# Moving a hybrid trunk's activation transfers to GpSimd's queue, its low halves and sums to VectorE, and its second modulation into the first feed-forward sweep

## The chip, the cores and the metric

One core of a Trainium2 chip runs the kernel: TensorE (matmuls, PE in the profile, with PEld for its weight loads), VectorE (DVE), ScalarE (ACT), GpSimd (POOL) and SyncE (SP), an on-chip memory of 128 partitions, eight matmul result banks, and a memory off the chip that transfers (DMA) reach. A transfer is issued by an engine's queue, in the order of that queue's program; an engine that comes to an instruction whose data or buffer is not ready waits, and with it all that stands behind. The metric is the device time of one execution in microseconds (us), the median of several.

## What is computed

Two layers over 1024 latent tokens and 256 context tokens of width 1024, all in fp32. Layer 0 mixes tokens by a convolution module, layer 1 by grouped-query attention (16 heads, 4 key heads); each is followed by a SwiGLU feed-forward part of width 2816. Each part is normalised before and after, and scaled, shifted and gated by a modulation: a linear map of SiLU(c) for latent tokens, of SiLU(c_ctx) for context tokens, six blocks of 1024 numbers per layer.

```
for i in range(2):
    mod_x = silu(c) @ w_mod[i] + b_mod[i]          # six blocks: sh, sc, g, shf, scf, gf
    mod_c = silu(c_ctx) @ w_mod[i] + b_mod[i]
    hx = rmsnorm(x, g0) * (1 + sc_x) + sh_x        # the same for ctx
    yx = conv_module(hx) if i == 0 else attention(hx, hc)
    x  = x + g_x * rmsnorm(yx, g1)                 # ctx too, in layer 0
    fx = rmsnorm(x, g2) * (1 + scf_x) + shf_x
    x  = x + gf_x * rmsnorm((silu(fx @ w1) * (fx @ w3)) @ w2, g3)
```

## The kernel before

**Data.** Activations stand with features on partitions and tokens along them, as 8 blocks of 128 features. The 1280 tokens form three pieces: C (256 context tokens), L and R (512 latent tokens each). A product of two fp32 matrices is made of three: each operand is split into a high half (rounded to fp32r) and a low half (the rest), and `mm3` (L149, its matmuls in L155, L156 and L157) adds high x high, high x low and low x high.

**Weights.** `wload` (L125) fetches a block of 128 x 1024 weights (512 KB) into one of two `wr` buffers over SP's queue, has ScalarE write the high half (`wh`, L132), and VectorE (L136) or GpSimd (L138) the low half (`wl`); there are three `wh` and three `wl`. `lo_dve` is the share of the low halves that goes to VectorE: 0 at the start, 1 from L914 on (convolution, layer norm, first feed-forward sweep), 0.5 from L1011 on, to the end of the kernel. Small tiles have rings too: `sb` of four buffers, `sm` of three; the halves of keys and queries lie in `sb` until their store has gone out.

**Transfers.** Nearly all are issued by SP, weights and activations in one queue: residual loads (L542), stores of the residual stream x1, x2, x3 and the output (L567, L990), keys (L731: 8 stores of a piece, each of 32 rows for 4 key heads), queries (L757: 4 stores per pair of projections), key loads (L763), query loads (L770, two buffers), attention results (L1048, and their loads L1079), cosines and sines (L726, L727), and the modulation's weights (L238). ScalarE issues some of the convolution's.

**Order of the work.** The program is written as generators; a foreground loop yields an estimate of its time, and `pump(budget)` lets generators in the background queue `bgq` issue as many steps as their own yields fit into that budget. So the order on each engine is largely that of the program. The stages:

1. Modulation of layer 0 (scale and shift by TensorE, the other 32 blocks by VectorE products beside the projections, `mod_dve`, L225), first normalisation, pointwise projections and the convolution, to about 385 us.
2. Layer norm, second pointwise projection, residual and second normalisation of C, L and R (`ln`, `pw2`, `post_pre`), to about 600 us.
3. First feed-forward sweep, over C and L together (L981): 22 up-steps with w1 and w3, and down-steps with w2 after each group of four. `pp("R")`, R's residual and normalisation, runs in its background. Matmul results have banks 0 to 4 and 7, statistics 5 and 6.
4. Second sweep, over R (L1012), with `early()` in the background: residuals of C and L, layer 1's modulation (all 48 blocks, `mod_dve` in room from the tiles T2 and T3), normalisation and keys and values of C, normalisation of L.
5. Handover: L's keys, values and queries beside R's residual and normalisation (L1015 to L1025), then R's keys, values and first query pair (L1026 to L1030). The first scores need all keys of a head back from off-chip memory.
6. Attention (`attn_stream`): per unit of a key head and 128 queries scores (L784), softmax numerators (L790 on VectorE, L792 on ScalarE), transposes (L802), halves (L805, L806) and values (L808, L809). At first R's other three query pairs run beside it; the second half of the units runs beside the output projection and the feed-forward sweep over L (L1111).
7. Output projection and feed-forward sweep over R (L1118), and the tail: the last residuals and the stores of the output.

**Sums.** `post` (L534) applies norm and gate to each of 8 feature blocks (VectorE, L550) and adds the residual (L553). `aid` names the blocks whose add goes to GpSimd: 6 of 8 in the handover, 4 of 8 from there on. `rsqrt` (L277) is a chain of small VectorE operations.

Of the kernel before, what the change touches and what calls it, by code (L numbers as in the profile page):

```python
# [15 lines left out]
P = 128  # L16
# [38 lines left out]
class Kern:  # L55
    def __init__(self, tc, es, a):
# [14 lines left out]
        self.aid = ()  # L71
# [153 lines left out]
    def mod_dve(self, l, fs, cr, raws, junk):  # L225


        nc = self.nc
        if l:
            self.cond_row(cr)  # L230

        def load(i):
            if i >= len(fs):
                return None
            raw = raws[i % len(raws)]
            if raw is None:
# [12 lines left out]
        for s in range(2 if l else 0):  # L249
            m = self.mod[l][s][:, 0:16 if s else 48]  # L250
            nc.vector.tensor_tensor(m, m, self.c["bmod"][:, l, 0:16 if s else 48], op=ALU.add)

    def mod_room(self, *tags):
        t = [self.T(g, [P, {"HS": 5312, "KB": 2656}.get(g, 4096)]) for g in tags]
        parts = [u[:, i:i + 1024] for u in t for i in range(2048 if u is t[0] else 0, u.shape[1] - 1023, 1024)]
        return t[0][:, 0:2048].rearrange("p (s d) -> p s d", s=2), parts[1:], parts[0]
# [277 lines left out]
    def post(self, l, i, y, yacc, xsrc, c0, segs, sink, xtag, kind="st"):  # L534
# [6 lines left out]
        def load(q):  # L541
            nc.sync.dma_start(xr[:, q % m:q % m + 2, :], xsrc[:, q:q + 2, c0:c0 + n])  # L542
# [4 lines left out]
        for k in range(KT):  # L547
# [5 lines left out]
            (nc.gpsimd if k in self.aid else nc.vector).tensor_tensor(yk, yk, xr[:, k % m, :], op=ALU.add)  # L553
# [5 lines left out]
    def post_pre(self, l, y, yacc, xsrc, xdst, c0, c1, dcol, xtag, ftags, box):  # L559
# [18 lines left out]
    def ffn(self, l, fs, ytags, htags, boxes, tanh=False, parts=1):  # L578
# [5 lines left out]
        ys = [self.T(t, [P, KT, n]) for t, n in zip(ytags, ns)]  # L584
# [135 lines left out]
    def qkv(self, h, col0, n, wk, want_q=True):  # L720
# [4 lines left out]
        if want_q:  # L725
            nc.sync.dma_start(wk[:, 0, :n], a["cos"][:, lat0:lat0 + n])  # L726
            nc.sync.dma_start(wk[:, 1, :n], a["sin"][:, lat0:lat0 + n])  # L727

        def ksink(i, v):
            for r in (i % 2, i % 2 + 2):  # L730
                nc.sync.dma_start(self.ksd[:, 32 * r:32 * r + 32, i // 2, col0:col0 + n], v)  # L731
# [19 lines left out]
        if want_q:  # L751
            for t in range(NKV):
# [4 lines left out]
                             lambda i, v: nc.sync.dma_start(  # L757
# [4 lines left out]
    def load_k(self, t, kt, c0=0, c1=TOK):  # L762
        self.nc.sync.dma_start(kt.bitcast(F32).rearrange("p (a t) -> p a t", a=2)[:, :, c0:c1],  # L763
                               self.ksd[t, :, :, c0:c1])

    def load_q(self, t, qt):
# [3 lines left out]
        nc.sync.dma_start(q, self.qsd[t, :, :, qt * P:(qt + 1) * P])  # L770
# [88 lines left out]
    def build(self):  # L859
# [70 lines left out]
        modg = self.mod_dve(0, range(16, 48), cr, (mraw, None), self.ps[:, 5:7].rearrange("p a b -> p (a b)"))  # L930
# [20 lines left out]
        for s in range(2):  # L951
            nc.vector.tensor_tensor(self.mod[0][s][:, 16:48], self.mod[0][s][:, 16:48], c["bmod"][:, 0, 16:48],
                                    op=ALU.add)
        self.derive(0, (1, 2, 3))
# [26 lines left out]
        for us in self.ffn(0, [(fv["C"][0], CTX), (fv["L"][0], 512)], ("HR", "T5"), ("KB", "HS"),  # L981
                           (zv["C"], zv["L"])):
            self.pump(us)
        self.drain()

        def final(l, y, src, dst, c0, c1, dcol, xtag, kind="st"):
            segs = segs_of(c0, c1)

            def sink(k):
                nc.sync.dma_start(dst[:, k, c0 - dcol:c1 - dcol], y[0][:, k, :])  # L990
# [20 lines left out]
        self.lo_dve = 0.5  # L1011
# [7 lines left out]
        self.aid = (1, 2, 3, 5, 6, 7)  # L1019
# [4 lines left out]
        self.aid = (1, 3, 5, 7)  # L1024
# [8 lines left out]
    def attention(self, final, qr):  # L1033
# [9 lines left out]
        def dst(q0):  # L1043
            def of(t, q):
                st = self.sb(256).rearrange("p (a q) -> p a q", q=P)

                def done():
                    nc.sync.dma_start(self.od[:, 2 * t:2 * t + 2, q * P:(q + 1) * P], st)  # L1048
# [175 lines left out]
```

## Time and profile before

| what | value |
|---|---|
| median of 3 runs | 3185.4 us (3184.72 to 3186.8) |
| the profiled execution | 3188.66 us; its span 3186.8 us |
| mean granted TensorE clock | 0.956 of full speed |
| TensorE busy | 2954.3 us, 93% (weight loads 2461.8) |
| VectorE busy | 1899.3 us, 60% |
| ScalarE busy | 1193.6 us, 37% |
| GpSimd busy | 352.9 us, 11%, 188 instructions |
| moved by SP's and ScalarE's queue | 328.91 MB, 31.8% of 16 engines' span |

How to read the rows: a group of instructions has its line, engine, operation, the tiles written and read (`wl<-wr,wh`), its count, then busy time and mean ns of one, then the engine's idle time just before them and what ended it. A timeline row has start and duration in us, and in brackets the idle time before it with what ended it (`<-DVE sm L683`: the end of VectorE's instruction in L683 that wrote `sm`). `SPq` is SP's queue; a merged row of it (x8) reaches from the first issue to the last. A window's row gives start and end, its length, the busy time of the five engines with their instructions, the granted clock, the DMA engines' mean share and GB/s. Times are from the span's start.

### The profile page before, as it was taken

To read this page: it belongs to the slowest core of one execution; us is meant where nothing else is said; L and a number is where in the kernel's file an instruction comes from. 1 tells how busy PE (TensorE), PEld (TensorE's weight loads), DVE (VectorE), ACT (ScalarE), POOL (GpSimd) and SP (SyncE) were. 2 spreads that over 40 slices of the span, in tenths; PEclk is the share of its full clock that TensorE was granted. 3 is DMA by queue.
4 is the path that set the end of the run, shared out by engine and by line. 5 is a ranking of instruction groups with operands and counts; after the bars stand their busy time and mean duration, and the time that the engine had idled before them with its cause. 6 is when DMAs were issued, how large, how long until landed. Compare 5 with 4: busy or idle time off the path is not lost. (4 is left out here: it accounts for less than half of the span.)

```text
span 3186.8 us, 39120 instructions
## 1 busy us (share of the span) xinstructions
PE 2954.3 (93%) x15210; PEld 2461.8 (77%) x15210; DVE 1899.3 (60%) x3026; ACT 1193.6 (37%) x1879; POOL 352.9 (11%) x188
## 2 busy tenths in 40 slices
PE   7899979899999999989966899989999999899997
PEld 5799878688888878778755677767777778778886
DVE  5877567742333379755564789866566653653335
ACT  5221245432111133233232588754545543332222
POOL 0000000000000012212221100021111112222222
PEclk9999959899999999999988899999999999899998
DMA  6544324322121257523334311222122133342332
GB/s 227 155 122 106 106 58 140 135 76 67 60 66 60 66 178 261 215 93 106 119 110 136 138 44 62 72 86 78 58 83 75 60 114 99 129 143 93 93 99 73
DMA packets 170425, 339.50 MB, mean 107 GB/s; under 512 B 30336, under 2 KB 83584, under 8 KB 169088
## 3 DMA queue, kind: packets, MB, share of 16 engines
q1 hardware_dynamic: 144128, 328.91, 31.8%
q10 hardware_dynamic: 26112, 8.10, 1.1%
q8 instruction: 119, 1.95, 0.3%
q14 instruction: 66, 0.54, 0.1%
HBM read 289.76 MB, written 41.81 MB: 104 GB/s over the span
## 5 line engine op out<-in xcount | busy, mean ns | idle before, releaser
L157 PE MATMUL ps<-T,wl 128*128 128x512 f32 (+1 forms) x2256 | 852.7, 378 | 33.9 <-DVE wl L136 32.6
L155 PE MATMUL ps<-T,wh 128*128 128x512 f32 (+1 forms) x2256 | 853.4, 379 | 9.2 <-ACT wh L132 7.0
L156 PE MATMUL ps<-T,wh 128*128 128x512 f32 (+1 forms) x2192 | 823.6, 376 | 1.8 <-DVE T L147 1.8
L132 ACT CAST wh<-wr 128x1024 fp32r<-128x1024 f32 x348 | 365.3, 1050 | 1098.1 <-PE ps L156 865.3
L138 POOL TENSOR_TENSOR wl<-wr,wh 128x1024 fp32r<-128x1024 f32 x123 | 301.5, 2452 | 2432.1 <-ACT wh L132 2232.2
L157 PEld LDWEIGHTS ps<-T,wl 128*128 128x128 f32 x2256 | 432.9, 192 | 113.5 <-DVE wl L136 35.4
L136 DVE TENSOR_TENSOR wl<-wr,wh 128x1024 fp32r<-128x1024 f32 x225 | 282.0, 1254 | 396.1 <-ACT wh L132 389.0
L155 PEld LDWEIGHTS ps<-T,wh 128*128 128x128 f32 x2256 | 432.4, 192 | 85.7 <-ACT wh L132 7.7
L156 PEld LDWEIGHTS ps<-T,wh 128*128 128x128 f32 x2192 | 419.5, 191 | 76.1 <-DVE T L147 3.3
L156 PE MATMUL ps<-HS,wh 128*128 128x512 f32 (+1 forms) x784 | 308.6, 394 | 3.0 <-DVE HS L147 3.0
L806 DVE TENSOR_TENSOR T<-ps,T 128x512 fp32r<-128x512 f32 x320 | 216.8, 687 | 126.4 <-ACT T L805 125.8
L157 PE MATMUL ps<-HS,wl 128*128 128x512 f32 (+1 forms) x720 | 281.5, 392 | 3.0 <-DVE wl L136 3.0
L155 PE MATMUL ps<-HS,wh 128*128 128x512 f32 (+1 forms) x720 | 281.6, 393 | 2.3 <-DVE sm L615 2.2
L805 ACT CAST T<-ps 128x512 fp32r<-128x512 f32 x320 | 185.9, 585 | 194.7 <-PE ps L802 170.5
L802 PE MATMUL ps<-cst,T 128*128 128x128 f32 x1100 | 193.2, 276 | 30.1 <-DVE T L806 29.8
L639 DVE TENSOR_TENSOR T<-ps,T 128x512 f32<-128x512 f32 (+1 forms) x168 | 110.1, 662 | 159.8 <-PE ps L157 159.3
L802 PEld LDWEIGHTS ps<-cst,T 128*128 128x128 f32 x1100 | 132.8, 141 | 79.1 <-DVE T L806 60.2
L790 DVE TENSOR_SCALAR_CACHE_REDUCE T<-ps,rq 128x1280 f32<-128x1280 f32 x110 | 169.9, 1545 | 28.8 <-PE ps L784 23.6
L615 DVE TENSOR_TENSOR sm<-sm,ps 128x256 f32<-128x256 f32 (+1 forms) x88 | 54.5, 619 | 207.9 <-PE ps L157 207.9
L156 PEld LDWEIGHTS ps<-HS,wh 128*128 128x128 f32 x784 | 150.1, 191 | 33.2 <-DVE HS L147 4.0
L792 ACT ACTIVATE T<-T,mn 128x1280 f32<-128x1280 f32 x110 | 150.4, 1367 | 62.9 <-DVE T L790 62.6
L784 PE MATMUL ps<-KB,q 128*128 128x512 f32 (+1 forms) x576 | 144.2, 368 | 23.3 <-DMA KB<-ksd 14.8
(183 smaller groups left out, 4189.6 us busy)
## 6 DMA issues: line engine op xcount, KB each, us to landing
wr<-in_w SPq DMA_DIRECT2D x264, 512.0 KB
T<-in_wmodT SPq DMA_DIRECT2D x48, 512.0 KB
wr<-in_pw SPq DMA_DIRECT2D x40, 512.0 KB
wr<-in_wmodT SPq DMA_DIRECT2D x16, 512.0 KB
KB<-in_wmodT SPq DMA_DIRECT2D x16, 512.0 KB
wr<-in_wq SPq DMA_DIRECT2D x16, 512.0 KB
qsd<-sb SPq DMA_DIRECT2D x32, 256.0 KB
q<-qsd SPq DMA_DIRECT2D x32, 256.0 KB
```

Of the source, the lines that this page charges most:

```text
L132: nc.scalar.copy(hi, raw)
L136: nc.vector.tensor_tensor(lo, raw, hi.bitcast(F32), op=ALU.subtract)
L138: nc.gpsimd.tensor_tensor(lo, raw, hi.bitcast(F32), op=ALU.subtract)
L155: nc.tensor.matmul(out[:, :n], lhsT=wh, rhs=xh, start=k == 0, stop=False)
L156: nc.tensor.matmul(out[:, :n], lhsT=wh, rhs=xl, start=False, stop=False)
L157: nc.tensor.matmul(out[:, :n], lhsT=wl, rhs=xh, start=False, stop=k == nk - 1)
L784: nc.tensor.matmul(sc[:, k0:k0 + w], lhsT=q[:, h, :], rhs=kt[:, p * TOK + k0:p * TOK + k0 + w], start=p == 0, stop=p == 1)
L790: nc.vector.tensor_scalar(out=pt, in0=sc, scalar1=rq[:, h:h + 1], scalar2=None, op0=ALU.mult, op1=ALU.min, accum_out=mn)
L792: nc.scalar.activation(pt, pt, AF.Exp, bias=mn, scale=-1.0, accum_out=sums[:, 0, h:h + 1])
L802: nc.tensor.transpose(tp[:, h * P:(h + 1) * P], Ps[h][:, j * P:(j + 1) * P], c["ident"])
L805: nc.scalar.copy(ph, tp)
L806: nc.vector.tensor_tensor(pl, tp, ph.bitcast(F32), op=ALU.subtract)
```

## The change

Three things, in one diff:

- **Queues.** Residual loads, the stores of x1, x2 and x3, keys and queries both ways, attention results both ways, cosines and sines are issued by GpSimd. SP keeps the weights, the convolution's and first-stage loads, the row of conditions (`cond_row`), and the output's stores of piece R (`eng=nc.sync`); the output's stores of L go to GpSimd.
- **Low halves and sums.** `aid` is gone: all residual adds are VectorE's. The line `lo_dve = 0.5` is gone: all low halves are VectorE's from the convolution on, except while R's queries run beside the first attention units, where `lo_dve = 0.0` gives them all to GpSimd.
- **Modulation.** Layer 0's `mod_dve` beside the projections stops at block 40. The blocks 40 to 47 of layer 0 and all 48 of layer 1 run behind `pp("R")` in the first feed-forward sweep, their weights loaded by GpSimd's queue into a part of the tile HR and, in turn, a `wr` buffer. The products' unused output takes the banks 5 and 6, so that sweep's matmuls have five banks and its statistics one; and its background's budget is half the foreground's time instead of all of it.

The diff, cut to its core:

```
-    def mod_dve(self, l, fs, cr, raws, junk):
-        if l:
-            self.cond_row(cr)
+    def mod_dve(self, l, fs, cr, raws, junk, q=None):
...
-            nc.sync.dma_start(raw, self.a["wmodT"][l, fs[i]])
+            (q or nc.sync).dma_start(raw, self.a["wmodT"][l, fs[i]])
...
-        for s in range(2 if l else 0):
-            m = self.mod[l][s][:, 0:16 if s else 48]
+        for s in range(2):
+            f0, f1 = fs[0], min(fs[-1] + 1, 16 if l and s else 48)
+            m = self.mod[l][s][:, f0:f1]
...
-            nc.sync.dma_start(xr[:, q % m:q % m + 2, :], xsrc[:, q:q + 2, c0:c0 + n])
+            nc.gpsimd.dma_start(xr[:, q % m:q % m + 2, :], xsrc[:, q:q + 2, c0:c0 + n])
-            (nc.gpsimd if k in self.aid else nc.vector).tensor_tensor(yk, yk, xr[:, k % m, :], op=ALU.add)
+            nc.vector.tensor_tensor(yk, yk, xr[:, k % m, :], op=ALU.add)
-            nc.sync.dma_start(xdst[:, k, c0 - dcol:c1 - dcol], y[:, k, :])
+            nc.gpsimd.dma_start(xdst[:, k, c0 - dcol:c1 - dcol], y[:, k, :])
...
-                nc.sync.dma_start(self.ksd[:, 32 * r:32 * r + 32, i // 2, col0:col0 + n], v)
+                nc.gpsimd.dma_start(self.ksd[:, 32 * r:32 * r + 32, i // 2, col0:col0 + n], v)
-                             lambda i, v: nc.sync.dma_start(
+                             lambda i, v: nc.gpsimd.dma_start(
...
-        self.nc.sync.dma_start(kt.bitcast(F32).rearrange("p (a t) -> p a t", a=2)[:, :, c0:c1],
+        self.nc.gpsimd.dma_start(kt.bitcast(F32).rearrange("p (a t) -> p a t", a=2)[:, :, c0:c1],
-        nc.sync.dma_start(q, self.qsd[t, :, :, qt * P:(qt + 1) * P])
+        nc.gpsimd.dma_start(q, self.qsd[t, :, :, qt * P:(qt + 1) * P])
...
-        modg = self.mod_dve(0, range(16, 48), cr, (mraw, None), ...)
+        modg = self.mod_dve(0, range(16, 40), cr, (mraw, None), ...)
...
-        self.set_banks(mm=[0, 1, 2, 3, 4, 7], st=[5, 6])
+        self.set_banks(mm=[0, 1, 2, 3, 7], st=[4])
+        def mods():
+            cr = room[:, 2048:4096].rearrange("p (s d) -> p s d", s=2)
+            junk = self.ps[:, 5:7].rearrange("p a b -> p (a b)")
+            self.cond_row(cr)
+            for l, f0 in ((0, 40), (1, 0)):
+                yield from self.mod_dve(l, range(f0, 48), cr, (room[:, 4096:5120], None), junk, nc.gpsimd)
+            self.derive(0, (3,))
+            self.derive(1, (0,))
+            self.derive(1, (1, 2, 3), (0,))
+        def rest_R():
+            yield from pp("R")
+            yield from mods()
-        self.bgq.append(pp("R"))
+        room = self.T("HR", [P, 5120])
+        self.bgq.append(rest_R())
-            self.pump(us)
+            self.pump(0.5 * us)
...
-            yield from self.mod_dve(1, range(48), *self.mod_room("T2", "T3"))
-            self.derive(1, (0,))
-            self.derive(1, (1, 2, 3), (0,))
-        self.lo_dve = 0.5
-        self.aid = (1, 2, 3, 5, 6, 7)
-        self.aid = (1, 3, 5, 7)
...
         self.set_banks(**beside)
+        self.lo_dve = 0.0
...
+        self.lo_dve = 1.0
         self.set_banks(mm=[6], st=[6], pt=[5], av=[7])
...
-                nc.sync.dma_start(o[:, 2 * q:2 * q + 2], self.od[:, 2 * q:2 * q + 2, q0:q0 + 512])
+                nc.gpsimd.dma_start(o[:, 2 * q:2 * q + 2], self.od[:, 2 * q:2 * q + 2, q0:q0 + 512])
```

More of the change, by code (lines that the diff above doesn't have):

```diff
@@ L70, in __init__ @@
         self.pace = 1
-        self.aid = ()
         self.rate, self.credit = 1.0, 0.0
@@ L248, in mod_dve @@
                 yield 1.13
-        for s in range(2 if l else 0):
-            m = self.mod[l][s][:, 0:16 if s else 48]
[L251 to L256, printed above, removed]
+        for s in range(2):
+            f0, f1 = fs[0], min(fs[-1] + 1, 16 if l and s else 48)
+            m = self.mod[l][s][:, f0:f1]
+            nc.vector.tensor_tensor(m, m, self.c["bmod"][:, l, f0:f1], op=ALU.add)
     def derive(self, l, which, streams=(0, 1)):
@@ L583, in ffn @@
         ns = [n for _, n in fs]
-        ys = [self.T(t, [P, KT, n]) for t, n in zip(ytags, ns)]
+        ys = [self.T(t, [P, KT, n]) if isinstance(t, str) else t for t, n in zip(ytags, ns)]
         hrs = [self.T(t, [P, GRP + 1, 2, n], F32R) for t, n in zip(htags, ns)]
@@ L929, in build @@
             nc.gpsimd.memset(self.U[:, :, o:o + n], 0.0)
-        modg = self.mod_dve(0, range(16, 48), cr, (mraw, None), self.ps[:, 5:7].rearrange("p a b -> p (a b)"))
+        modg = self.mod_dve(0, range(16, 40), cr, (mraw, None), self.ps[:, 5:7].rearrange("p a b -> p (a b)"))
         nc.sync.dma_start(self.craw, a["wwin"][0])
@@ L950, in build @@
             pass
[L951 to L954, printed above, removed]
+        self.derive(0, (1, 2))
         self.set_banks(mm=[0, 1, 2, 3], st=[5, 6, 4, 7])
@@ L1121, in attention @@
                 self.banks["st"] = [4, 5, 6, 7]
-                self.aid = (1, 3, 4, 6)
-                tails.append(final(1, zR[0], self.x3d, out, CTX + 512, CTX + 768, CTX, "T6"))
+                tails.append(final(1, zR[0], self.x3d, out, CTX + 512, CTX + 768, CTX, "T6", eng=nc.sync))
                 next(tails[0])
-        tails.append(final(1, zR[1], self.x3d, out, CTX + 768, TOK, CTX, "T4"))
+        tails.append(final(1, zR[1], self.x3d, out, CTX + 768, TOK, CTX, "T4", eng=nc.sync))
         next(tails[1])
```

14 lines of the change are left out of this document (6 added, 8 removed).

## The prediction

> **What bounds the kernel now.** I read the granted clock, then the busy time by stage, then TensorE's waits, then each engine's timeline where TensorE stood still. The stage windows come first (start:end, length, busy us of TensorE, its weight loads, VectorE, ScalarE and GpSimd with instruction counts, granted clock, DMA share, GB/s):
>
> ```profile
> 385.00:600.00 215.00, 176.13 (x856) 155.92 (x857) 161.05 (x331) 106.89 (x191) 0.00 (x0) 0.78 0.35 116
> 600.00:1175.00 575.00, 575.00 (x3286) 507.02 (x3285) 222.82 (x334) 141.48 (x210) 8.89 (x3) 1.00 0.25 79
> 1175.00:1600.00 425.00, 400.05 (x1801) 329.58 (x1800) 286.78 (x427) 128.63 (x179) 88.70 (x35) 0.96 0.48 160
> 1600.00:1757.00 157.00, 98.18 (x458) 80.78 (x456) 88.00 (x191) 45.40 (x70) 25.90 (x14) 0.82 0.38 131
> ...
> 2200.00:2640.00 440.00, 425.30 (x2136) 336.46 (x2136) 264.55 (x368) 220.67 (x342) 58.83 (x34) 1.00 0.24 78
> 2640.00:2820.00 180.00, 168.77 (x718) 136.04 (x717) 100.67 (x147) 59.62 (x79) 43.52 (x19) 0.95 0.35 114
> ```
>
> The first feed-forward sweep (600 to 1175) has no idle TensorE: nothing can be won there, only lost. The handover from layer 0 to attention (1600 to 1757) holds 58.8 us of idle at a clock of 0.82; the sweep over piece R before it 25.0 us; the layer norm stage 38.9 us; the sweep beside the attention 14.7 us; the stage from 2640 on 11.2 us. Two waits lead TensorE's list (total, times, longest):
>
> ```profile
> PE ps L687 <- DVE sm L683: 38.4, 10, 11.5
> PE ps L157 <- DVE wl L136: 35.6, 8, 10.6
> ```
>
> VectorE is named, but in the handover it was itself waiting. TensorE's four long stops, in brackets the idle time:
>
> ```profile
> 1629.00 1.87 PE L687 MATMUL ps<-cst,sm 128*128 128x4 f32 x8 [11.54 <-DVE sm L683]
> ...
> 1668.02 0.80 PE L157 MATMUL ps<-T,wl 128*128 128x512 f32 x1 [10.61 <-DVE wl L136]
> ...
> 1688.15 1.87 PE L687 MATMUL ps<-cst,sm 128*128 128x4 f32 x8 [10.84 <-DVE sm L683]
> ...
> 1757.39 1.22 PE L784 MATMUL ps<-KB,q 128*128 128x512 f32 x2 [14.80 <-DMA KB<-ksd]
> ```
>
> Behind the first and third stands ScalarE, which works in order and was held by a weight's landing and by the `sb` buffers of the key stores:
>
> ```profile
> 1617.12 0.63 ACT L328 ACTIVATE sb<-T 128x512 f32<-128x512 f32 x1 [4.45 <-DMA ksd<-sb]
> 1623.41 1.04 ACT L132 CAST wh<-wr 128x1024 fp32r<-128x1024 f32 x1 [5.66 <-DMA wr<-in_wq]
> ...
> 1682.67 1.04 ACT L132 CAST wh<-wr 128x1024 fp32r<-128x1024 f32 x1 [18.56 <-DMA wr<-in_wq]
> ```
>
> These weights were late because of SP's order: they were issued after stores of keys and queries.
>
> ```profile
> 1597.42 13.56 SPq L731 DMA_DIRECT2D ksd<-sb  x8
> 1611.08 4.05 SPq L131 DMA_DIRECT2D wr<-in_wq  x2
> ...
> 1670.22 2.97 SPq L131 DMA_DIRECT2D wr<-in_wq  x1
> ```
>
> The second stop is VectorE, held in front of a low half by a query store that had not let go of its `sb` buffer:
>
> ```profile
> 1666.05 0.69 DVE L147 TENSOR_TENSOR sb<-T,sb 128x512 fp32r<-128x512 f32 x1 [4.34 <-DMA qsd<-sb]
> ```
>
> The fourth is the same store seen from the end: the DMA share and the GB/s in 40 slices of the window 1726 to 1762.
>
> ```profile
> DMA  0000212222222223222238995222222569999999
> GB/s 0 0 0 7 23 18 64 100 100 102 102 105 100 100 102 123 102 100 102 102 114 218 405 419 230 102 100 102 93 102 105 82 214 437 441 444 398 373 405 405
> ```
>
> While only key stores run the share stays at 2 tenths and about 102 GB/s; weights and loads on either side reach 405 to 444. These stores use about a quarter of the engines.
>
> **The change part by part.** *Activations' transfers to GpSimd.* SP keeps the weights and the early loads, so a weight is issued as soon as one of its two `wr` buffers is free.
>
> Handover. The third stop goes (10.84), and of the first the weight's part (5.66); after such a stop TensorE runs slowly: a clock of 0.82 costs 17.7 us on the stage's 98.2 us of matmuls, of which I put half on the four long stops, 2 us each, so 4 us more. That is 20.5 us off. Late next is VectorE: its 88.0 us of work here, plus the adds and low halves below, fit in what is left.
>
> The second and fourth stops hang on the stores' speed, which no row shows for GpSimd's queue. One end: 102 GB/s as now, nothing gained, since a store still holds its buffer. The other: all engines as in the 405 GB/s slices, both stops go, 25.4 us and 4 us of slow clock. I take the middle, 14 us off, as both rows are of this same place and neither is nearer.
> The Trainium skill, "DMA: Bandwidth & Descriptors", section "Why a DMA increments its semaphore by 16 and not by 1", says how many engines a copy gets: the largest number up to 16 that divides the slowest dimension of both sides; the 4 of `ksd` gives 4 engines, and the 102 GB/s agree. It adds that SP's copies always take the lowest-numbered engines, and GpSimd's go round all 16; no run here shows that yet. By it the term is the far end, 29 us, and the sum 15 us lower.
>
> Sweep over R. At 1431 a weight was late behind eight key stores of the context:
>
> ```profile
> 1431.25 0.79 PE L155 MATMUL ps<-T,wh 128*128 128x512 f32 x1 [6.30 <-ACT wh L132]
> ```
>
> This goes. Of the stage's other 18.7 us of idle and the 16 us that a clock of 0.96 costs on 400 us of matmuls I take a third, 11.7, because the modulation's VectorE work leaves this stage. 18 us off, from 6 to 41.
>
> From 2640 the same order holds weights behind the `x3d` stores:
>
> ```profile
> 2738.64 1.04 ACT L132 CAST wh<-wr 128x1024 fp32r<-128x1024 f32 x1 [5.21 <-DMA wr<-in_w]
> ```
>
> About half the stage's idle: 6 us off, from 0 to 11. In 385 to 600 VectorE is busy 161 of 215 us and weights wait for its low halves in order: 4 off, from 0 to 12.
>
> What is paid: each transfer now occupies GpSimd in order. Behind a store that waits for its data stand the next query load, the copy of the softmax sums (L815), and, while attention runs beside the queries' projection, six low halves that TensorE waits for. The query load is asked for one unit ahead, so it is covered; for the six halves I take 0, from 10 us off to 10 us on, since that stage also gives VectorE back three or so of them.
>
> *Low halves on VectorE.* One on GpSimd (the page's row, whole span), and one on VectorE in the first sweep (700 to 1100, 48 weights in 400 us):
>
> ```profile
> L138 POOL TENSOR_TENSOR wl<-wr,wh 128x1024 fp32r<-128x1024 f32 x123 | 301.5, 2452 | 2432.1 <-ACT wh L132 2232.2
> ```
>
> ```profile
> L136 DVE TENSOR_TENSOR wl<-wr,wh 128x1024 fp32r<-128x1024 f32 x48 | 58.8, 1226 | 139.3 <-ACT wh L132 139.3
> ```
>
> Each costs VectorE 1.23 us more. But VectorE pays for GpSimd's halves already. The feed-forward's own low half, in the sweep without GpSimd (700 to 1100) and in the one with it (2200 to 2600):
>
> ```profile
> L147 DVE TENSOR_TENSOR HS<-sm,HS 128x512 fp32r<-128x512 f32 x16 | 11.0, 684 | 0.0
> ```
>
> ```profile
> L147 DVE TENSOR_TENSOR HS<-sm,HS 128x512 fp32r<-128x512 f32 x13 | 26.3, 2024 | 3.1 <-ACT HS L144 2.8
> ```
>
> It is 1.34 us longer, 13 times: 17.4 us back for some 20 halves at 1.23, so VectorE's sum stays even, and it has 175 us free of the 440. The latency matters: the matmuls that follow wait for that half. I take 7 us, half of the stage's idle; from 0 to 14.7.
>
> *Sums on VectorE.* In the handover, layer 1's first residual and the tail GpSimd did part of the adds:
>
> ```profile
> 1607.93 0.68 DVE L553 TENSOR_TENSOR T<-T,T 128x512 f32<-128x512 f32 x1
> ...
> 1608.09 8.87 POOL L553 TENSOR_TENSOR T<-T,T 128x512 f32<-128x512 f32 x6 [4.10 <-DVE T L550]
> ```
>
> Six adds take 8.87 us there, 4.1 on VectorE, whose chain ends no later. In the residual at 2140 four adds cost VectorE 2.7 us less what it waited for GpSimd: 1.5 on. In the tail four half-width adds lie open: 1.5 on.
>
> *Second layer's modulation behind the first sweep.* 80 products (16 for the last block of layer 0, 64 for layer 1), of which 64 leave the R sweep. From 1180 to 1320 they show
>
> ```profile
> L245 DVE CUSTOM_DVE_ANT_0 T<-T,T x42: 1207/1225/3437, 1185.7 to 1319.8; 128x1024 f32<-128x1024 f32 x42
> ```
>
> 80 x 1.23 = 98 us on a VectorE that has 352 us free there, so the work is hidden. The rows are not sure to be: every second one takes one of the two `wr` buffers that the weights use. A load and its use, at SP's pace:
>
> ```profile
> 598.84 5.96 SPq L131 DMA_DIRECT2D wr<-in_w  x3
> ```
>
> ```profile
> 602.13 1.05 ACT L132 CAST wh<-wr 128x1024 fp32r<-128x1024 f32 x1 [3.33 <-DMA wr<-in_w]
> ```
>
> 3.3 + 1.2 = 4.5 us for a buffer, 2.25 us a row with two. The pump asks for 15.36 x 0.5 / 1.13 = 6.8 products per pair of weights, which at 48 weights in 400 us takes TensorE 16.7 us: one per 2.45 us, and in the last 32 rows each product is a row. If GpSimd's issue adds 1 us, a row takes 2.75 and 32 rows fall back 10 us, part of it covered by the weights held ready. I take 5 us on, from 0 to 25. The five banks for matmuls instead of six cost nothing: an up-step needs four, and the fifth is free by then.
>
> The sum: -20.5 - 14 - 18 - 6 - 4 + 0 - 7 + 1.5 + 1.5 + 5 = -61.5. The profiled execution took 3188.7 us (span 3186.8), so 3127; the median of the runs lies 3.3 lower: **3124 us**.
>
> **The rivals.** *Stores spread over the engines*: the far end above, and GpSimd sends them with no weight ahead. The key and query stores of the attention stage gain too, and the 10 us there: 3124 - 15 - 10 = 3099. For it: the quarter share is plain in the row. Against: the choice of engines may be the copy's, not the queue's. The round over 16 engines (the skill's page above) would be this case.
>
> *VectorE hides it*: weights come early and wait for in-order VectorE, whose low halves stand behind normalisation. Only the third stop, the context's key stores and the contention stay won: 10.8 + 6.3 + 7 = 24, and 3 of the adds are lost: 3164. For it: L687's waits name VectorE; against: the 18.56 us wait is a DMA's.
>
> *Modulation holds the first sweep*: 25 on instead of 5: 3144. It decides if a row's load through GpSimd takes over 3.7 us (2 x 2.45 - 1.22).
>
> *GpSimd's queue becomes the bound of the handover*, the slower side. Between 1600 and 1757 the code issues there 16 key stores, 16 query stores, 8 residual stores and 7 loads, 47 in all. The sum leaves the handover 122 us, so an issue of over 2.6 us decides, and over 3.9 us the kernel is slower than before. At 4.9 us, two of GpSimd's low halves, 47 take 230 us, 108 more: 3232. For it: a simple GpSimd operation takes 2.45 us here. Against: SP got all 47 out in this window beside its weights; no GpSimd transfer is in this trace. The Trainium skill, "SBUF — State Buffer", section "SBUF: two separate sides", warns that GpSimd cannot write its transfers' descriptors while VectorE runs an operation that uses both its ports; no run here shows it.
>
> *The change does not do what it says* where weights wait for their two buffers and not for SP's order; that is the second rival's time.
>
> **How the numbers follow.** Forecast 0.42, with 3100 to 3148 as its own range; spread stores 0.24; VectorE 0.14; modulation 0.10; GpSimd's queue 0.10. About 0.2% (6 us) can be told from no change. Slower: the last, less its mild half, plus the unexpected: 0.09; same 0.04; faster 0.87. The range takes in the first four and the bounds of the stores: 3075 to 3168.
>
> **What would show it.** Right: no weight load's wait over 5 us on ScalarE between 1600 and 1757; HS at L147 near 0.68 us in every sweep; the handover's window near 122 us; the R sweep at a clock above 0.98. Stores right if the slices beside key stores alone rise above 102 GB/s. Wrong: a TensorE below 575 of 575 us in the first sweep, waits on L245's rows, or GpSimd busy without a gap in the handover.

## The result, and the profile after

The changed kernel takes 3155.0 us (median of 4, 3144.8 to 3160.9), the kernel before 3186.0 us beside it: a ratio of 0.990, 95% interval 0.9873 to 0.9926. So it is faster, by 1% or 31 us and not by 61.5. The profiled execution is the fastest of the four, 3144.8 us with a span of 3143.0; the stages below are its own, 43.9 us under the profiled execution of before, and the median lies 10.2 us above it.

The stage windows after, in the columns of the windows before (stages shifted with the kernel):

```profile
600.00:660.00 60.00, 46.20 (x271) 40.33 (x269) 50.95 (x101) 22.87 (x35) 6.59 (x13) 0.92 0.37 123
...
780.00:840.00 60.00, 47.63 (x249) 40.34 (x248) 38.60 (x61) 7.96 (x12) 9.52 (x18) 0.90 0.67 213
...
900.00:1198.00 298.00, 298.00 (x1693) 262.16 (x1692) 109.76 (x173) 64.78 (x95) 2.88 (x4) 1.00 0.23 69
1198.00:1600.00 402.00, 392.89 (x1821) 325.84 (x1821) 206.30 (x334) 129.44 (x180) 26.41 (x42) 0.99 0.37 115
1600.00:1735.00 135.00, 92.25 (x437) 76.64 (x435) 81.42 (x192) 45.27 (x69) 33.23 (x43) 0.83 0.55 155
2180.00:2607.00 427.00, 423.83 (x2142) 337.06 (x2141) 270.48 (x391) 221.81 (x344) 29.28 (x46) 1.00 0.25 81
2607.00:2777.00 170.00, 164.25 (x720) 132.70 (x719) 101.20 (x165) 59.62 (x79) 10.83 (x18) 0.99 0.36 118
```

The first sweep, full before, now has idle TensorE in its first half, while the new products run, and is full again from 900 on. Every later stage shown here is fuller than before.

Where the time went is read best from the weights. ScalarE makes the high half of 348 weights, the same ones in every kernel here and, at the places of the table, in the same order (the context's four of keys and values come some thirty places earlier, between 1108 and 1583, where the modulation has moved); the start of such a cast, less the start of the same cast in the kernel before, is how far a kernel is ahead (minus) at that place. Places are times of the kernel before; from the last row on the difference stays to the end. Each column is one execution, and those of the changed kernel lie up to 16 us apart, so a difference of a few us between two columns means little.

| at | changed | without part 3 | queues only | low halves only | half pace | keys, queries on SP | idle work on GpSimd |
|---|---|---|---|---|---|---|---|
| 605, first sweep begins | -12.6 | -12.6 | -13.8 | -2.0 | -13.6 | -8.9 | -12.2 |
| 1108, modulation done | +23.3 | -11.9 | -13.1 | -2.0 | -4.1 | +27.9 | -11.5 |
| 1583, sweep over R done | -0.5 | -39.8 | -12.3 | -26.6 | -27.0 | +5.4 | -13.7 |
| 1771, attention begins | -21.9 | -59.8 | -7.2 | -29.8 | -46.5 | -3.9 | -18.5 |
| 2207, half of it done | -19.2 | -60.0 | +1.6 | -27.1 | -45.9 | -4.3 | -11.7 |
| 2634, sweep over L done | -33.1 | -72.3 | +2.7 | -43.3 | -58.4 | -18.0 | -9.9 |
| 2823 | -43.7 | -81.3 | +0.7 | -56.6 | -68.9 | -28.9 | -11.4 |

The first column is the change; the others are experiments told below. It loses 35.9 us in the first sweep and gains 23.8 in the sweep over R, 21.4 in the handover, 13.9 beside the attention and 10.6 after it.

TensorE's first stop in the first sweep, and its four long stops of the handover as they are now (timeline of after, idle time in brackets):

```profile
660.51 0.58 PE L154 MATMUL ps<-T,wh 128*128 128x256 f32 x1 [14.31 <-ACT wh L131]
...
1644.15 1.87 PE L679 MATMUL ps<-cst,sm 128*128 128x4 f32 x8 [4.20 <-DVE sm L675]
1656.11 0.79 PE L156 MATMUL ps<-T,wl 128*128 128x512 f32 x1 [10.09 <-DVE wl L135]
1673.38 1.87 PE L679 MATMUL ps<-cst,sm 128*128 128x4 f32 x8 [6.88 <-DVE sm L675]
...
1735.12 1.22 PE L776 MATMUL ps<-KB,q 128*128 128x512 f32 x2 [12.78 <-DMA KB<-ksd]
```

The first of the handover's stops fell from 11.54 to 4.20 and the third from 10.84 to 6.88; the second and the fourth, which hang on stores, shrank little (10.61 and 14.80 before). The key stores at the end did spread over the DMA engines (after, 1706 to 1742, share and GB/s in 40 slices):

```profile
DMA  1000053469947899997888542139678999893000
GB/s 55 27 14 0 9 43 36 60 105 132 124 96 183 264 305 251 224 251 246 229 251 233 157 165 114 41 73 259 255 73 328 496 410 421 371 405 123 9 0 0
```

Seven to nine tenths of the engines are busy now where it was two, at some 250 GB/s where it was 102, part of it weights; and the scores still wait 12.78 us. From the first key store's issue to that of the load that waits for them it is 21.3 us, 24.5 before.

Weights are still late in the handover, though none stands behind a store on SP. The latest one, as ScalarE saw it, and two rows of the page of after (KB of a transfer, median us from issue to landing):

```profile
1725.61 1.04 ACT L131 CAST wh<-wr 128x1024 fp32r<-128x1024 f32 x1 [13.58 <-DMA wr<-in_wq]
```

```profile
wr<-in_w SPq DMA_DIRECT2D x264, 512.0 KB, 3.6
wr<-in_wq SPq DMA_DIRECT2D x16, 512.0 KB, 6.5
```

That weight was issued at 1711.69, inside the burst of eight key stores, and landed 13.8 us later. From 1597 to 1730 the eleven weights issued while key or query stores were under way landed 6.1 to 13.8 us after their issue, the four others after 3.3 to 3.5. The times coincide; no run here takes the stores away to show that they are the cause.

### The profile page after: what moved, and what is told of

The parts are those of the page before. It is cut to its first block, busy times and chain, and to the rows that moved or that the text cites. A ratio compares the mean times of both kernels' runs of the same rounds, so it can differ in the third digit from the quotient of the medians.

```text
span 3143.0 us, 39119 instructions
## 1 busy us (share of the span) xinstructions
PE 2942.5 (94%) x15210; PEld 2455.0 (78%) x15210; DVE 1895.5 (60%) x3169; ACT 1192.6 (38%) x1879; POOL 233.9 (7%) x360
## 5 line engine op out<-in xcount | busy, mean ns | idle before, releaser
L154 PE MATMUL ps<-T,wh 128*128 128x512 f32 (+1 forms) x2256 | 850.9, 378 | 21.4 <-ACT wh L131 15.1
L135 DVE TENSOR_TENSOR wl<-wr,wh 128x1024 fp32r<-128x1024 f32 x340 | 416.1, 1225 | 401.5 <-ACT wh L131 390.7
L156 PEld LDWEIGHTS ps<-T,wl 128*128 128x128 f32 x2256 | 430.9, 191 | 104.4 <-DVE wl L135 28.9
L782 DVE TENSOR_SCALAR_CACHE_REDUCE T<-ps,rq 128x1280 f32<-128x1280 f32 x110 | 170.0, 1545 | 28.9 <-PE ps L776 24.2
L155 PEld LDWEIGHTS ps<-HS,wh 128*128 128x128 f32 x784 | 149.5, 191 | 29.0 <-DVE HS L146 0.2
L776 PE MATMUL ps<-KB,q 128*128 128x512 f32 (+1 forms) x576 | 144.6, 371 | 21.4 <-DMA KB<-ksd 13.5
L154 PEld LDWEIGHTS ps<-HS,wh 128*128 128x128 f32 x720 | 136.1, 190 | 36.0 <-ACT sm L606 8.3
```

The source lines that it names most:

```text
L135: nc.vector.tensor_tensor(lo, raw, hi.bitcast(F32), op=ALU.subtract)
L154: nc.tensor.matmul(out[:, :n], lhsT=wh, rhs=xh, start=k == 0, stop=False)
L155: nc.tensor.matmul(out[:, :n], lhsT=wh, rhs=xl, start=False, stop=False)
L156: nc.tensor.matmul(out[:, :n], lhsT=wl, rhs=xh, start=False, stop=k == nk - 1)
L776: nc.tensor.matmul(sc[:, k0:k0 + w], lhsT=q[:, h, :], rhs=kt[:, p * TOK + k0:p * TOK + k0 + w], start=p == 0, stop=p == 1)
L782: nc.vector.tensor_scalar(out=pt, in0=sc, scalar1=rq[:, h:h + 1], scalar2=None, op0=ALU.mult, op1=ALU.min, accum_out=mn)
```

## The experiments

Each was timed in five rounds beside the kernel before; ratios are to it, with their 95% interval. The code shows edited lines only.

**What holds the first sweep.** Two theories met: A, transfers and buffers make weights late; B, VectorE works in order and waits for rows (a row is the 512 KB of the modulation's weights that one or two products need). Four edits of the changed kernel:

```
-            self.cond_row(cr)                      # first
+            self.cond_row(cr, nc.gpsimd)
```
```
-  self.mod_dve(..., (room[:, 4096:5120], None), ...)          # second; the third has both
+  self.mod_dve(..., (room[:, 4096:5120], self.sbb[:, :1024]), ...)
```
```
-  yield from self.mod_dve(l, range(f0, 48), cr, ...)          # fourth
+  for u in self.mod_dve(l, range(f0, 48), cr, ...): yield 2 * u
```

> The changed kernel with one transfer moved: the row of conditions for the second modulation is loaded by GpSimd's queue and not by SP's. Theory A: the first sweep's 36 us are two things, and the first is this row: on SP it waits 23.6 us for R's last residual, the weights behind it are late, and TensorE stands 14.31 us at 660 and then runs slowly, some 18 us in all. Then this kernel takes 18 us off the changed one: a ratio of about 0.9845 to the kernel before, and no stop at 660. Theory B: the rows of the modulation themselves hold VectorE and the weights, and the row of conditions is only seen first; then the stop stays or moves to the next weights, and the ratio stays near 0.990.

Measured: 3151.9 us, 0.9899 (0.9886 to 0.9913). The stop stays (14.42 us at 664). Theory A's first half falls: the row of conditions is not what makes the weight late.

> The changed kernel, but the modulation's second row buffer is two of the four sb buffers (unused there) and not one of the weights' two wr buffers. Theory A: the second half of the 36 us (11 us idle between 790 and 860 and a clock of 0.87) comes from weights that find one of their two buffers taken by a row; own room gives 17 us back, ratio about 0.985, and the stop at 660 stays. Theory B: VectorE works in order and waits for rows that land 4.4 us after GpSimd issues them, its low halves behind it; then own room changes nothing between 790 and 860, ratio 0.990.

Measured: 3150.6 us, 0.9902 (0.9888 to 0.9917). In this kernel and the next the four `sb` buffers are parts of one tile, handed out in turn. Their output is off by a tenth (why was not traced), and the layer norm stage is 15 us longer, so their ratios say little; only the first sweep is read here, which issues the same work but for the row's buffer. The stop at 660 is gone, and the sweep loses 18 us and not 36. So a row in a weight buffer made the first stop. In the changed kernel GpSimd's second row took a `wr` buffer at 633 while its product stood far back in VectorE's program, and SP's next weight waited for that product:

```profile
633.06 0.54 POOL L234 DMA_DIRECT2D wr<-in_wmodT  x1 [0.33 <-issue]
```

```profile
SPq L130 <- DVE mod L241: 23.6, 1, 23.6
```

But the stretch from 720 to 840 lost as much as before, against A (this kernel's waits and window there; TensorE is 10.9 us short):

```profile
DVE ps L241 <- DMA sb<-in_wmodT: 19.1, 13, 4.2
DVE ps L241 <- DMA HR<-in_wmodT: 15.8, 12, 2.7
```

```profile
720.00:840.00 120.00, 109.06 (x592) 93.39 (x591) 83.71 (x135) 20.76 (x31) 19.02 (x36) 0.96 0.67 211
```

VectorE's work and its waits for rows fill 118.6 of the 120 us, and ScalarE waited only 6.2 us for weights.

> Both edits, own row buffers and the row of conditions on GpSimd's queue. Theory A: the two causes add up, the first sweep is whole again (TensorE busy throughout between 600 and 900): 36 us off the changed kernel, a ratio of about 0.979. Theory B: at least half of the 36 us stays, ratio 0.984 or more.

Measured: 3152.2 us, 0.990 (0.9886 to 0.9915). By its casts 19 of the 36 us stay in the first sweep, as B said; the ratio holds the 15 us of the layer norm stage too.

> The changed kernel, but each product of the moved modulation asks for twice the foreground's time, so a row comes every 4.9 us of the sweep and not every 2.45; buffers and queues as changed. If a row in a wr buffer costs a fixed piece of the weights' time, as theory A says in its simplest form, the second 17 us stay and the ratio stays at 0.990, spread over a longer stretch. If it is the pace, rows asked for faster than two buffers turn over, the stops between 790 and 860 go and the ratio falls to 0.985; the stop at 660 stays in both.

Measured: 3121.2 us, 0.980 (0.9787 to 0.9814): 34 us off, more than either expected, with one stop of 7.00 us left in the sweep. So the pace matters. What it does is seen in VectorE's waits (total, times, longest) and the window, both from 720 to 840: first after, then with half the pace.

```profile
DVE ps L241 <- DMA wr<-in_wmodT: 26.6, 12, 5.1
DVE ps L241 <- DMA HR<-in_wmodT: 18.1, 10, 3.5
```

```profile
720.00:840.00 120.00, 107.63 (x596) 93.51 (x595) 75.70 (x119) 21.80 (x33) 16.92 (x32) 0.95 0.60 189
```

```profile
DVE ps L241 <- DMA wr<-in_wmodT: 21.9, 6, 4.3
```

```profile
720.00:840.00 120.00, 120.00 (x700) 106.45 (x699) 65.83 (x99) 25.40 (x37) 6.87 (x13) 1.00 0.39 115
```

After: 75.7 us of work and 44.7 us of waiting for rows make 120.4 of 120 us. VectorE is full, with 37% of its time spent waiting, and TensorE falls short by 12.4. In this kernel the shared buffers have a part as well: ScalarE waited 52.4 us for weights there, and TensorE's longest stop, 8.1 us, was for ScalarE. At half the pace the two make 87.7, and TensorE has all 120.

The fifth kernel took the `wr` buffers out of it altogether, and gave a row 7 us:

```
+  nc.gpsimd.dma_start(raw, a["wmodT"][l, f])       # raw = room[:, 4096:5120], alone
+  yield 3.2
+  for s in ...: nc.vector.tensor_tensor_reduce(out=junk, in0=raw, ...)
```

> The changed kernel with the moved modulation in one row buffer of its own (the part of HR that it has already) and none of the weights' wr buffers; a row is loaded right after the product before it, asks for 3.2 us of the background's budget, and its product comes only then, some 7 us later. Theory C, formed from the first four runs: the first sweep loses by two things, a wr buffer held from 633 to 655 by a row whose product stood far back in VectorE's queue, and rows asked for faster than they land; both are gone here, so the 9 us that the slower pace alone still lost go too: about 3112 us, ratio 0.977, TensorE 575 of 575 us in the sweep. Rival: rows of 512 KB slow the weights' transfers themselves; then some of the 9 us stays and the ratio is 0.980.

Measured: 3146.1 us, 0.9867 (0.9853 to 0.9881). Theory C falls; the rival missed too, as the sweep loses 32 us by the casts. The pump runs once per pair of weights, so two or three rows come in a burst, and with one buffer VectorE takes a product, then waits while the next row is loaded (waits and window from 720 to 840 of this kernel):

```profile
DVE ps L981 <- DMA HR<-in_wmodT: 50.2, 17, 5.2
```

```profile
720.00:840.00 120.00, 111.89 (x617) 97.68 (x616) 68.50 (x109) 20.84 (x30) 8.99 (x17) 0.96 0.43 132
```

50.2 + 68.5 = 118.7 of 120 us, and TensorE is short again, with no weight buffer touched. Its last product comes at 1004, that of the half pace at 1011, so the pace alone is not it. In the second and fifth kernel, where no row lies in a weight buffer, the sweep loses because VectorE's work and its waits for rows fill the time; in the fourth they leave room, and it does not.

**What each part is worth alone.** Three kernels: the change without its third part (modulation, banks and pump of that sweep as before), the first part alone, the second part alone.

```
-        modg = self.mod_dve(0, range(16, 40), ...)            # without part 3
+        modg = self.mod_dve(0, range(16, 48), ...)
...
+            yield from self.mod_dve(1, range(48), ...)        # again in early()
```

> The changed kernel without its third part: the second layer's modulation is back in the sweep over R and the last block of layer 0's beside the projections, rows over SP; queues, low halves and sums as changed. If the move is worth what the prediction put on it in the sweep over R (11.7 us) and costs 36 us in the first sweep, this takes 24 us off: 3131 us, ratio 0.983. Rival: the sweep over R gained by the context's key stores alone, no longer ahead of weights on SP; then the whole 36 us come back, 3119 us, ratio 0.979. Third: SP's loads for the modulation hold weights there again, and it is no better than the changed kernel, 0.990.

Measured: 3107.5 us, 0.9757 (0.974 to 0.9774). Better than all three expectations. The third part costs the changed kernel 1.4%, 46 us; by the table 35 of 38 in the first sweep. And the sweep over R, with the modulation in it, gains 27.9 us where the changed kernel gained 23.8: that taking the modulation out of that sweep saves anything is not seen.

```
-            nc.sync.dma_start(...)         # the kernel before, part 1: all its transfers
+            nc.gpsimd.dma_start(...)
```

> The kernel before with its activations' transfers on GpSimd's queue and nothing else changed: half the low halves from the sweep over R on, and part of the sums, stay on GpSimd. If the order on SP is the main gain, the stages that showed weights behind stores give the same here as in the changed kernel (layer norm stage 12, context's keys 15, handover 21, from 2640 on 10 us): 3128 us, ratio 0.982. Rival: GpSimd works in order, so its low halves (2.45 us each) stand behind stores that wait for their data, TensorE waits for them, and less than half of that is left: 3160 us or more, ratio 0.992 or above; then the low halves' move is what makes the queue's move pay.

Measured: 3189.5 us, 0.9999 (0.9988 to 1.001): nothing. The layer norm stage's 12 us are there, the sweep over R gains nothing though its key stores are off SP, the handover and the attention lose 5 and 9. That is inside the rival's bound (3160 us or more); that low halves behind waiting stores are the reason is not shown by this run.

```
-        self.lo_dve = 0.5                  # the kernel before, part 2; aid gone as in the change
...
+        self.lo_dve = 0.0                  # beside the first attention units
+        self.lo_dve = 1.0                  # after them
```

> The kernel before with only its second part: all low halves and residual sums on VectorE from the sweep over R on (GpSimd alone beside the first attention units), every transfer on SP as before. The prediction put 7 us on it, less 3 for the sums: 3182 us, ratio 0.999. The theory now, from the run with the queues alone (no gain) and the one without the modulation's move (81 us): the stages after the first sweep gain by the low halves, 28 us in the sweep over R, 12 beside the attention, 9 from 2640 on; the layer norm stage's 12 stay with the queues; in the handover the two need each other, so 0 to 20 there. That gives 3137 to 3117 less nothing else: ratio about 0.980 to 0.985. Rival: both parts are needed everywhere, as weights behind stores on SP hide what early low halves give: ratio 0.995.

Measured: 3130.5 us, 0.9821 (0.9808 to 0.9835), as expected: 56 us from the part that the prediction put at 7 less 3. Part 1 on top of it gives another 0.6%, 20 us, most of it in the layer norm stage and the handover.

**Why the low halves matter.** VectorE's rows in the sweep over R (1110 to 1560: count, busy us, mean ns), in the kernel before and in the change without its third part:

```profile
L245 DVE CUSTOM_DVE_ANT_0 T<-T,T 128x1024 f32<-128x1024 f32 x50 | 72.9, 1457 | 2.6 <-DMA T<-in_wmodT 1.9
L136 DVE TENSOR_TENSOR wl<-wr,wh 128x1024 fp32r<-128x1024 f32 x38 | 52.6, 1384 | 37.4 <-ACT wh L132 37.4
L147 DVE TENSOR_TENSOR HS<-sm,HS 128x512 fp32r<-128x512 f32 x22 | 36.1, 1641 | 13.3 <-ACT HS L144 13.3
L639 DVE TENSOR_TENSOR T<-ps,T 128x512 f32<-128x512 f32 x44 | 29.8, 687 | 35.3 <-PE ps L157 35.3
```

```profile
L135 DVE TENSOR_TENSOR wl<-wr,wh 128x1024 fp32r<-128x1024 f32 x79 | 96.5, 1223 | 53.2 <-ACT wh L131 51.8
L241 DVE CUSTOM_DVE_ANT_0 T<-T,T 128x1024 f32<-128x1024 f32 x50 | 61.1, 1222 | 5.2 <-DMA T<-in_wmodT 4.6
L636 DVE TENSOR_TENSOR T<-ps,T 128x512 f32<-128x512 f32 x50 | 34.2, 690 | 30.9 <-PE ps L156 30.7
...
L146 DVE TENSOR_TENSOR HS<-sm,HS 128x512 fp32r<-128x512 f32 x23 | 15.8, 686 | 0.7 <-ACT HS L143 0.7
```

Operations with two operands in on-chip tiles were longer while GpSimd made low halves (1457 to 1222, 1384 to 1223, 1641 to 686 ns); the one that reads a matmul result is not (687 and 690). Two theories of what the low halves on GpSimd cost: its operations lengthen VectorE's, or a low half of 2.45 us is late itself. The next kernel keeps all low halves on VectorE and lets GpSimd work for nothing:

```
             nc.vector.tensor_tensor(lo, raw, hi.bitcast(F32), op=ALU.subtract)
+            nc.gpsimd.tensor_tensor(self.gj, raw[:, :512], hi[:, :512].bitcast(F32), op=ALU.subtract)
```

> The changed kernel without the modulation's move (3107.5 us), and beside each VectorE low half from the sweep over R on GpSimd subtracts half a weight block for nothing (128x512 of the same weight and high half, into a tile that no one reads): as much GpSimd work as the kernel before had there. No matmul waits for it. If what the low halves cost on GpSimd is what its operations do to VectorE's beside them (the feed-forward's own low half 684 ns alone, 2024 ns beside them), most of the gain of these stages goes again: 25 us or more, ratio 0.983 or above, and that row is near 2 us again. If it is the low half's own 2.45 us and its place behind GpSimd's other work, nothing is lost: ratio 0.976.

Measured: 3177.6 us, 0.9969 (0.9957 to 0.998): 70 of the 81 us are gone, as the first theory's "25 or more". In the table this kernel is at 605 where the one without part 3 is, and loses in every stage after it what the low halves had brought. Its rows in the same stretch:

```profile
L135 DVE TENSOR_TENSOR wl<-wr,wh 128x1024 fp32r<-128x1024 f32 x74 | 101.6, 1375 | 39.4 <-ACT wh L131 38.2
L244 DVE CUSTOM_DVE_ANT_0 T<-T,T 128x1024 f32<-128x1024 f32 x50 | 73.8, 1477 | 2.6 <-DMA T<-in_wmodT 2.0
...
L148 DVE TENSOR_TENSOR HS<-sm,HS 128x512 fp32r<-128x512 f32 x23 | 25.8, 1121 | 0.7 <-ACT HS L145 0.7
```

```profile
L137 POOL TENSOR_TENSOR gj<-wr,wh 128x512 f32<-128x512 f32 x72 | 142.5, 1980 | 729.3 <-ACT wh L131 705.7 <-issue 20.1 <-DMA wr<-in_w 3.2
```

No matmul reads `gj`; from 1110 to 2823 ScalarE waited for it twice and VectorE once, 5.2 us in all. The products and low halves are as long as in the kernel before; the feed-forward's own low half is longer again (1121 ns, 1285 beside the attention) but not near 2 us. The idle work was more than the kernel before had: 345.8 us from 1110 to 2823, where low halves and sums there took 251.

It also held something that the expectation left out, the weight buffers that it reads (SP's queue, 1110 to 1560):

```profile
SPq L130 <- POOL gj L137: 40.1, 34, 2.9
```

ScalarE waited 61.7 us for weights in that stretch, 10.1 without the idle work. So the 70 us need not be the contention's alone: late weights, and the transfers that GpSimd issues behind its idle work, may hold a part, and this run does not tell them apart up to the attention. Beside the attention (2207 to 2634 of the kernel before) it does: no engine waited for a weight there, the waits for other transfers are 4.5 us in all where they were 3.0, and the stage takes 429 us where it took 415. VectorE's 380 instructions of it, the same in both, take 276.7 us and not 262.3. So there longer VectorE rows cost the 14 us.

**What the stores cost.** Three kernels: the changed one with key and query stores back on SP; one without part 3 and with each key half stored once instead of twice and its rows loaded twice; the same with a fifth `sb` buffer.

```
-                nc.gpsimd.dma_start(self.ksd[...], v)         # and the same for qsd
+                nc.sync.dma_start(self.ksd[...], v)
```

> The changed kernel with only the stores of keys and queries back on SP. If the order on SP is what they cost, the 21 us of the handover and 15 us of the context's keys are lost again: 3191 us, ratio 1.001. Rival: in the changed kernel the weights of the handover wait for their two buffers and for the transfer itself, as long as before, and the stores land no sooner from GpSimd; then most of the handover's gain has another source (residual loads and stores, sums) and this takes about 3165 us, ratio 0.993.

Measured: 3159.7 us, 0.9909 (0.9896 to 0.9923), near the rival's 0.993 and not told apart from the changed kernel. In the table it gains 22.5 us in the sweep over R with the context's key stores ahead of weights again, so those were not the reason there; the handover's gain falls from 21.4 to 9.3. At its end TensorE waits longer for the keys:

```profile
1752.47 0.79 PE L776 MATMUL ps<-KB,q 128*128 128x512 f32 x1 [16.10 <-DMA KB<-ksd]
```

```
-            for r in (i % 2, i % 2 + 2):
-                nc.gpsimd.dma_start(self.ksd[:, 32 * r:32 * r + 32, ...], v)
+            r = i % 2
+            nc.gpsimd.dma_start(self.ksd[:, 32 * r:32 * r + 32, ...], v)
...
+        for z in (0, 64):                  # load_k: both halves of the partitions from the same 64 rows
```

> The changed kernel without the modulation's move (3107.5 us), and each half of a key is stored once and not twice (4 stores of a piece and not 8, 1 MB and not 2 MB for 512 tokens); the loads of a head fetch the 64 rows twice. If the first scores wait for the landing of the stores (10.9 us of idle TensorE), and weights and residual loads share the engines with them, the handover gets 8 to 12 us shorter: 3097 us, ratio 0.972. Rival: a store's landing is the last one's own time and GpSimd's order, not the bytes ahead; then 0 to 3 us, ratio 0.975.

Measured: 3107.4 us, 0.9749 (0.9736 to 0.9763), no difference. The wait for the keys fell (10.88 to 7.40 us), and the handover is 6 us shorter in the table's measure (26.0 won, not 20.0); beside the attention it is given back (5.6 won between 2000 and 2634, not 12.1). What takes it there stays open.

> The same with a fifth sb buffer. In the run without the modulation's move VectorE and ScalarE stood 5 us at 1610 for an sb buffer that a query store still held, and TensorE 10.8 us at 1618 behind them. If the buffers' number is the limit, a fifth takes most of that stop away: 5 to 10 us below the kernel with single key stores, ratio 0.969 to 0.970. Rival: the next store's buffer is held just as long, and the stop only moves; no difference.

```
-  tag="sb", name="sb", bufs=4
+  tag="sb", name="sb", bufs=5
```

Measured: 3102.3 us, 0.9732 (0.9717 to 0.9747), the fastest kernel here, though its interval overlaps that of the kernels with 3107: neither expectation is decided by the time. The stop at 1619, first with four and then with five buffers:

```profile
1619.83 0.80 PE L156 MATMUL ps<-T,wl 128*128 128x512 f32 x1 [11.16 <-DVE wl L135]
```

```profile
1614.19 0.80 PE L156 MATMUL ps<-T,wl 128*128 128x512 f32 x1 [8.46 <-DVE wl L135]
```

Only 2.7 us of the stop are gone. VectorE no longer waits for a store's buffer there, but ScalarE does (3.57 us at 1611, 5.01 with four), and VectorE waits 3.41 us for ScalarE: the wait has mostly moved, as the rival said.

## Why the prediction came out as it did

The sign was right and 3155 lies in the range, but the forecast missed by 31 us and lies outside the 3100 to 3148 that it gave its own mechanism. That it fell into the wide range is partly luck: by the table the first sweep and the handover came out 44 us worse than forecast, and four other stages 25 us better, most of it by the low halves, which were priced at next to nothing.

- *Modulation, +5 (0 to 25), measured +35.9.* This is the step that failed. The prediction saw that VectorE had 352 us free and called the products hidden; it priced the rows as transfers (4.5 us for a buffer). It left out that VectorE waits for a row in order, and that these waits fill it as work does (44.7 us beside 75.7 of work in 120). Its own condition for the rival *modulation holds the first sweep*, a row's load over 3.7 us, was met: GpSimd's rows land 4.0 to 4.4 us after their issue (medians of the page). That rival's 25 was still too small; it left out the buffer held from 633 on, some 18 us by the second run.
- *Sweep over R, -18, measured -23.8*, for neither of its two reasons. With the stores off SP alone it loses 0.8 us, and with the modulation still in it the two other parts gain 27.9. It is the end of GpSimd's low halves (24.6 with these alone).
- *Low halves and sums, -7 and +3, measured -56 alone.* The prediction read the contention in one row, beside the attention, and used it there; it did not look for it in the sweep over R, where the same row was 1641 ns and the products 1457. The 13.9 us beside the attention are twice its 7, the 10.6 from 2640 on are this part too (13.3 with it alone, 2.0 with the queues alone) and not weights behind `x3d` stores.
- *Handover, -34.5, measured -21.4.* Queues alone: 5.1 us lost; low halves alone: 3.2 won; both: 20.0. Of the two stops at L687 the first shrank by 7.3 us where 5.66 was forecast, the third by 4.0 where all 10.84 was to go. The sign "no weight load's wait over 5 us on ScalarE" did not hold: five weights still came 6.3 to 13.6 us late. The prediction laid such waits to SP's order alone; off that order, weights issued beside stores took 6.1 to 13.8 us to land.
- *Stores, -14 of these, between 0 and 29.* At most the 12 us by which the handover is longer with them on SP. The rule of the Trainium skill ("DMA: Bandwidth & Descriptors", section "Why a DMA increments its semaphore by 16 and not by 1") fits the share, two tenths from SP and, the weights' part included, seven to nine from GpSimd. The 29 us that the prediction made of it did not come, since the stops behind the stores hardly moved. So *stores spread over the engines* was true and not worth its price.
- *Layer norm stage, -4, measured -11.8*, by the queues, as argued. *Attention, sums, tail:* 0, +1.5, +1.5 forecast; the attention with its residual's sums +2.7, the tail 0 measured.
- *GpSimd's queue as the bound* fell: an issue takes 0.53 to 0.8 us, and the 40 in the handover's window took 26 of its 135 us.

## What to carry to other kernels

Count an in-order engine's waits for a moved operation's data as its work: an engine with half its time free can be full. A helper engine's work can be paid in the longer operations of its neighbour: compare one row's mean with and without it in every stage before costing a move. And test the parts of a change alone; here one part hid in the other's gain, and leaving the third out is worth more than the whole change.

## What the runs showed of the hardware

GpSimd operations lengthen VectorE operations whose two operands are both in on-chip tiles (686 to 1641 ns, 1222 to 1457), and not those that read a matmul result (690 and 687). The Trainium skill, "SBUF — State Buffer", section "SBUF: two separate sides", says that the two engines share a pair of ports, which a VectorE operation with two SBUF inputs (against a GpSimd one that reads SBUF) or a GpSimd one takes for its whole length; these rows agree. GpSimd itself pays: its 128x512 subtraction took 1.27 us at the shortest and 2.02 in the mean of 236. GpSimd's transfers cost VectorE nothing that its rows show: in the first sweep its low halves take 1224 ns beside GpSimd's rows, 1226 without them.

With seven to nine tenths of the DMA engines busy and not two, the keys were stored in 21.3 us and not 24.5, and half the bytes took only 3.5 us off the wait for them. A 512 KB weight load issued beside such stores landed 6.1 to 13.8 us after its issue, and 3.3 to 3.5 without them.
